# Down products of a feed-forward network in the seven-product form, for 18 of 22 feature tiles

## The chip, the cores and the metric

The kernel runs on one core of a Trainium2 chip. The metric is the device time of one execution in microseconds (us). TensorE (PE) multiplies, VectorE (DVE) and ScalarE (ACT) do elementwise work, GpSimd (POOL) here mostly issues DMAs that add what they bring to what is there, SyncE (SP) issues the plain loads.

## What is computed

A trunk of two layers over 512 positions of 1024 channels. Each layer has a feed-forward network (FFN), a mixer (pooling, a Fourier map and attention side by side) and a second FFN; a norm follows at the end. The change touches the FFNs alone:

```
def rmsnorm(x, g):
    y = xf * lax.rsqrt(jnp.mean(xf * xf, axis=-1, keepdims=True) + NORM_EPS)
    return (y * g.astype(jnp.float32)).astype(x.dtype)
def swiglu(x, w_gate, w_up, w_down):
    return (jax.nn.silu(x @ w_gate) * (x @ w_up)) @ w_down
...
for l in range(DEPTH):                       # 2
    h = rmsnorm(x, ffn1_norm[l])
    x = x + 0.5 * swiglu(h, ffn1_w_gate[l], ffn1_w_up[l], ffn1_w_down[l])
    ...
    h = rmsnorm(x, ffn2_norm[l])
    x = x + 0.5 * swiglu(h, ffn2_w_gate[l], ffn2_w_up[l], ffn2_w_down[l])
```

w_gate and w_up are 1024 x 2816, w_down is 2816 x 1024; all data is float32.

## The kernel before

**Operands in two halves.** Each float32 operand is split into a rounded part (hi, type float32r) and the rest (lo). A product is three matmuls: hi x hi, lo x hi, hi x lo (`mm3`, lines 106 to 109). `split` (102 to 104) makes hi on ACT and lo on DVE. Names: `hi`/`lo` are weights, `xh`/`xl`/`xo` the halves of the FFN's input, `ah`/`al` those of the hidden tiles.

**Layout.** x lies transposed in eight tiles of 128 channels x 512 positions. The hidden layer has 22 feature tiles of 128, handled in 11 pairs. `CHUNKS` (43) cuts the pairs into chunks of 4, 4 and 3. For each chunk the gate/up products of its pairs run first, and then the down products of its feature tiles into all eight output tiles, which are added to x (`ffn`, 577 to 602).

**The seven-product form.** A unit (class `Unit`, 448 to 510) is the gate and up product of one pair. The unit takes the input tiles in pairs too, and the 512 positions in two halves, so that gate and up are 2 x 2 block products, for which seven block products suffice instead of eight (Winograd's form of Strassen's). They are numbered 1 to 7; their inputs are the tiles themselves (1, 2, 3: `own` splits) and sums of tile halves (4 to 7: `ta`, `tb` in `joined`, 357 to 376), and their weights are sums of blocks too. Each product has 256 columns per matmul. They gather in four PSUM banks `qe`, `qa`, `qb`, `qg`. `head` runs products 5 and 1, `middle` 6, 7 and 2, `tail` 4 and 3; five DVE additions (`y`, `v`, `w`) combine the banks. The tail of a unit is written behind the head of the next one. The combined gate and up are multiplied with the norm's factor into tiles `t`, ACT applies silu, DVE multiplies gate with up (lines 506, 507; "gate" in the text), and `hidden` splits the result into `ah` and `al`.

**The plain down products.** For each output tile m one weight operand of up to 1024 columns is consumed, and every feature tile of the chunk costs three matmuls of 512 columns into bank `dn`; line 600 adds half of the bank to x. In the last chunk each finished output tile is fed to the next norm (`nxt.feed`): it makes that norm's operands and squares.

**Weights.** `raw` and `operand_of` write down, ahead of all, the loads and the operands in their order. SP loads a raw tile into one of 7 stage buffers; where a block sum is wanted, POOL adds a second block by an accumulating DMA (`plus`, line 167), and after an operand has been split, another (`then`, line 190) turns the stage tile into the next sum. `produce` splits a stage tile into one of four hi and four lo buffers; `operand` produces three operands ahead (`AHEAD`). So the hi and lo of an operand can be made only when PE has finished with the operand four before it.

**Order.** The program's order is not the code's: a scheduler interleaves the instructions of each engine, and each engine then runs its own list in order. Four hi and lo buffers, eight PSUM banks and one pool of 54 general tiles (`g`) bound how far it can go.

The lines that the change and the prediction's steps touch are 43, 122 to 155, 357 to 376, 448 to 532 and 577 to 602.

Of the kernel before, what the change touches and what calls it, by code (L numbers as in the profile page):

```python
# [32 lines left out]
P = 128  # L34
D = 1024
S = 512
# [6 lines left out]
CHUNKS = ((0, 4), (4, 8), (8, 11))  # L43
# [23 lines left out]
def build(tc, xt, gu, dn, qk, wv, wfa, wo, pw, fw, small, lamv, alibi, dft_c, dft_s, out):  # L67
# [3 lines left out]
    with (  # L71
# [50 lines left out]
        for l in range(L):  # L122
            for n in range(2):
                i = 2 * l + n
                if n:
# [3 lines left out]
                    for x in ORDER:  # L129
                        if x in src:  # L130
                            for z in range(2):
                                operand_of(raw(src[x][:, z * 1024 : (z + 1) * 1024]), eng=V if x in ON_VECTOR else None)
                for c0, c1 in CHUNKS:
                    tail = []
                    for u in range(c0, c1):
                        a11, a21, a22, a12 = [gu[i, u][:, q * 1024 : (q + 1) * 1024] for q in range(4)]
                        if not raws:
                            for x in (a11, a12, a21, a22):
                                operand_of(raw(x))
                            continue  # L140
                        t, t11 = raw(a21, plus=a22), raw(a11)
                        t12, t22 = raw(a12), raw(a22)
                        if u == 1 and i == 0:
                            for x, then in ((t11, a21), (t, a11), (t11, None), (t, a12), (t12, None)):
                                operand_of(x, then=then)
                            tail = [(t22, None), (t, None)]
                            continue
                        for x, then in [(t, a11), (t11, a21)] + tail + [(t, a12), (t11, None), (t12, None)]:
                            operand_of(x, then=then)
                        tail = [(t22, None), (t, None)]  # L150
                    for x, then in tail:
                        operand_of(x, then=then)
                    for m in range(KT):
                        w = 2 * (c1 - c0) * P
                        operand_of(raw(dn[i, m][:, 2 * c0 * P : 2 * c1 * P], w), w)
# [55 lines left out]
        X = [cp.tile([P, S], F32, name=f"x{k}") for k in range(KT)]  # L211
# [128 lines left out]

        class PairNorm(Norm):
# [15 lines left out]
            def joined(self, b1, b2, res=None):  # L357

                c0, c1 = slice(0, TH), slice(TH, S)
                ta, tb = g(name="ta"), g(name="tb")  # L360
# [641 lines left out]
```

## Time and profile before

| what | value |
|---|---|
| time, median of 3 runs | 1839.99 us (1838.53 to 1840.71) |
| the profiled execution's own time | 1840.45 us |
| its span, first to last instruction | 1838.7 us |
| mean granted TensorE clock | 0.987 |
| ACT, POOL busy | 884.9 us, 204.8 us |
| HBM read | 258.99 MB |

In the profile's rows the names stand as out<-in; "busy" adds the instructions of an engine, and "idle before" is the time its queue stood still just ahead of an instruction, with what released it. PE is the matmul row, PEld the loading of the stationary operand, which overlaps it. A matmul's own duration is modelled and overlaps the next one's, so distances between starts say more.

### The profile page before, as it was taken

What the parts mean: (1) busy time and instruction counts of PE and PEld (TensorE: products, weight loads), DVE (VectorE), ACT (ScalarE), POOL (GpSimd) and SP (SyncE); (2) the same over time, 40 slices, a digit from 0 to 9 for tenths busy, and PEclk for the clock granted to TensorE, in tenths of its full rate; (3) what the DMA queues carried; (4) which work ended last, traced back from release to release, by engine and by line L of the source; (5) the groups of instructions that cost most, each with busy time, mean ns of one, the idle gap of its engine ahead of it and who ended that gap; (6) DMA issues with size and microseconds to landing.
All of it is one profiled execution on the core that took longest, in us unless ns stands there. A gap on an engine that the chain in (4) does not pass through costs nothing.

```text
span 1838.7 us, 28135 instructions
## 1 busy us (share of the span) xinstructions
PE 1773.4 (96%) x11286; PEld 1602.7 (87%) x11286; DVE 1278.8 (70%) x2004; ACT 884.9 (48%) x1223; POOL 204.8 (11%) x242
## 2 busy tenths in 40 slices
PE   8999999999899999999999999999988999999997
PEld 7889989877678989989899899998766899899895
DVE  7765846868679765847887477477776887477474
ACT  7433424468646533424554244244875554244243
POOL 1101001001101101001010010100111110010101
PEclk9999999999899999999999999999998999999998
DMA  7757757545625857857677586665444467586661
GB/s 240 184 149 161 197 133 175 143 124 131 138 67 130 192 160 154 202 130 179 152 169 188 136 195 173 138 169 155 115 118 104 102 158 188 133 200 162 140 158 46
DMA packets 81778, 279.69 MB, mean 152 GB/s; under 512 B 9200, under 2 KB 12784, under 8 KB 81648
## 3 DMA queue, kind: packets, MB, share of 16 engines
q0 software_dynamic: 29376, 106.97, 33.6%
q1 hardware_dynamic: 48528, 166.73, 28.0%
q10 hardware_dynamic: 3744, 4.21, 0.8%
q8 instruction: 88, 1.44, 0.3%
q14 instruction: 42, 0.34, 0.1%
HBM read 258.99 MB, written 2.10 MB: 142 GB/s over the span
## 4 chain that ended last, share of the span: by engine, by line
PE 79%; DVE 6%; ACT 5%; DMA 4%; issue 4%; POOL 1%; SPq 0%; ACTq 0%; DVEq 0%; POOLq 0%
PE dn L107 8%; PE dn L108 8%; PE dn L109 8%; PE qg L462 4%; PE qg L464 4%; PE qg L463 4%; PE qe L463 4%; PE qe L464 4%; PE qe L462 4%; PE qa L464 4%; PE qa L463 4%; PE qa L462 4%; DMA st<-in_gu 4%; PE qb L463 2%; PE qb L464 2%
## 5 line engine op out<-in xcount | busy, mean ns | idle before, releaser
L103 ACT ACTIVATE hi<-st 128x1024 fp32r<-128x1024 f32 (+2 forms) x420 | 432.9, 1035 | 621.4 <-PE dn L108 223.6
L104 DVE TENSOR_TENSOR lo<-st,hi 128x1024 fp32r<-128x1024 f32 (+2 forms) x420 | 500.7, 1194 | 194.5 <-ACT hi L103 193.0
L108 PE MATMUL dn<-al,hi 128*128 128x512 f32 x704 | 274.6, 390 | 0.0
L109 PE MATMUL dn<-ah,lo 128*128 128x512 f32 x704 | 274.2, 389 | 0.0
L107 PE MATMUL dn<-ah,hi 128*128 128x512 f32 x704 | 271.9, 392 | 0.5
L462 PE MATMUL qg<-xh,hi 128*128 128x256 f32 x688 | 196.9, 286 | 6.1 <-ACT hi L103 3.2
L462 PE MATMUL qe<-xh,hi 128*128 128x256 f32 x688 | 196.9, 286 | 4.3 <-DVE nv L328 2.3
L463 PE MATMUL qg<-xh,lo 128*128 128x256 f32 x688 | 196.1, 285 | 0.9 <-DVE lo L104 0.9
L464 PE MATMUL qg<-xl,hi 128*128 128x256 f32 x688 | 196.1, 285 | 0.0
L464 PE MATMUL qe<-xl,hi 128*128 128x256 f32 x688 | 195.6, 284 | 0.1
L463 PE MATMUL qe<-xh,lo 128*128 128x256 f32 x688 | 195.4, 284 | 0.0
L190 POOL DMA_DIRECT2D st<-in_gu x129 | 116.1, 901 | 673.1 <-DVE lo L104 600.3
L600 DVE SCALAR_TENSOR_TENSOR x<-dn,x 128x512 f32<-128x512 f32 x96 | 66.2, 690 | 168.6 <-PE dn L109 168.6
L107 PEld LDWEIGHTS dn<-ah,hi 128*128 128x128 f32 x704 | 131.3, 188 | 31.9 <-ACT ah L103 5.9
L108 PEld LDWEIGHTS dn<-al,hi 128*128 128x128 f32 x704 | 132.2, 188 | 29.0 <-DVE al L104 2.4
L109 PEld LDWEIGHTS dn<-ah,lo 128*128 128x128 f32 x704 | 132.2, 188 | 26.9
L462 PEld LDWEIGHTS qg<-xh,hi 128*128 128x128 f32 x688 | 133.3, 194 | 7.4 <-ACT hi L103 3.4
L462 PEld LDWEIGHTS qe<-xh,hi 128*128 128x128 f32 x688 | 132.4, 192 | 8.1 <-ACT hi L103 4.9
L463 PEld LDWEIGHTS qg<-xh,lo 128*128 128x128 f32 x688 | 133.5, 194 | 1.1 <-DVE lo L104 1.1
L463 PEld LDWEIGHTS qe<-xh,lo 128*128 128x128 f32 x688 | 132.6, 193 | 1.3 <-issue 0.7
L464 PEld LDWEIGHTS qg<-xl,hi 128*128 128x128 f32 x688 | 133.4, 194 | 0.0
L464 PEld LDWEIGHTS qe<-xl,hi 128*128 128x128 f32 x688 | 132.6, 193 | 0.4 <-DVE xl L104 0.3
(274 smaller groups left out, 3923.3 us busy)
## 6 DMA issues: line engine op xcount, KB each, us to landing
st<-in_gu SPq DMA_DIRECT2D x175, 512.0 KB, 4.6
st<-in_gu POOLq DMA_DIRECT2D x172, 512.0 KB, 5.7
st<-in_dn SPq DMA_DIRECT2D x64, 512.0 KB, 4.2
lo<-st POOLq DMA_DIRECT2D x32, 512.0 KB, 5.0
st<-in_dn SPq DMA_DIRECT2D x32, 384.0 KB, 3.2
st<-in_qk SPq DMA_DIRECT2D x16, 512.0 KB, 3.7
st<-in_wo SPq DMA_DIRECT2D x16, 512.0 KB, 3.8
st<-in_wv SPq DMA_DIRECT2D x8, 512.0 KB, 4.9
```

The lines of the kernel that those rows point to most:

```text
L103: A.activation(hi, src, AF.Copy)
L104: (lo_eng or V).tensor_tensor(lo, src, f(hi), SUB)
L107: T.matmul(o, lh, rh, start=start, stop=False)
L108: T.matmul(o, lh, rl, start=False, stop=False)
L109: T.matmul(o, ll, rh, start=False, stop=stop)
L190: G.dma_start(t[:, 0:w], then, accum_op=ADD)
L462: T.matmul(o, wh[:, s], xh, start=start and p == 0 and z == 0, stop=False, **k)
L463: T.matmul(o, wl[:, s], xh, start=False, stop=False, **k)
L464: T.matmul(o, wh[:, s], xl, start=False, stop=stop and p == NK - 1 and z == 1, **k)
L600: V.scalar_tensor_tensor(X[m], b, 0.5, X[m], MUL, ADD)
```

## The change

The down products of the first nine pairs (18 of 22 feature tiles) take the seven-product form as well. `CHUNKS` becomes three chunks of three pairs and one of two; the last one keeps the plain down products. For a chunk of three pairs two `DownUnit`s run, each of four output tiles: the pairs of feature tiles are what the input pairs are in gate/up, and the two halves of positions are the same. So each product has 3 pairs x 2 x 3 = 18 matmuls of 256 columns, and a chunk has two units of seven products where it had eight plain operands.

- For each pair, the two hidden tiles are no longer split as `ah` and `al`, but made into the inputs of the seven products (`joined`: four half sums, then splits of `ta`, `tb` and the tiles).
- The unit ahead of the down products is written differently (`flush`): its gate and split are done by halves of positions, in the order in which they become ready.
- The first `DownUnit` of a chunk (`all_but_tail`) runs product 1, product 5 of the first two pairs, product 2, product 5 of the last pair, then 6 and 7. Its tail comes behind the head of the second one, and the tail of the second behind the head of the next chunk's first gate/up unit.
- Each `DownUnit` combines its banks by the same five additions and updates x by four additions of 2 x 256 columns.
- The weights of the down products are packed like those of gate/up: four blocks of 768 columns per unit, four loads and four accumulating DMAs, and seven splits of 768 columns, where a plain output tile had one load and one split.
- Two x tiles share one allocation (`XW`).

```
-CHUNKS = ((0, 4), (4, 8), (8, 11))
+CHUNKS = ((0, 3), (3, 6), (6, 9), (9, 11))
+NSEVEN = 9
...
+                def seven(src, w, plain=False, flush=False, special=False):
+                    nonlocal tail
+                    a11, a21, a22, a12 = src
...
+                    if flush:
+                        t11, t = raw(a11, w), raw(a21, w, a22)
+                    else:
+                        t, t11 = raw(a21, w, a22), raw(a11, w)
+                    t12, t22 = raw(a12, w), raw(a22, w)
...
+                    elif flush:
+                        use = tail + [(t11, a21), (t, a11), (t12, None), (t, a12), (t11, None)]
+                    else:
+                        use = [(t, a11), (t11, a21)] + tail + [(t, a12), (t11, None), (t12, None)]
+                    for x, then in use:
+                        operand_of(x, raws[x][1], then=then)
+                    tail = [(t22, None), (t, None)]
...
+                    if c1 <= NSEVEN:
+                        for o in range(2):
+                            q0 = [2 * P * (NSEVEN * q + c0) for q in range(4)]
+                            seven([d7[i, o][:, q : q + w] for q in q0], w, False, o == 0)
+                        continue
...
+        def own(b1, b2, res):
+            c0, c1 = slice(0, TH), slice(TH, S)
+            if b1 is not None:
+                one = g(F32R, name="xo")
+                split(b1[:, c0], one[:, c0], one[:, c1])
+                res[1] = one[:, c0], one[:, c1]
+            if b2 is not None:
+                hi, lo = g(F32R, name="xh"), g(F32R, name="xl")
+                split(b2, hi, lo)
+                res[2], res[3] = (hi[:, c0], lo[:, c0]), (hi[:, c1], lo[:, c1])
...
             def tail(self):
                 self.product(self.qg, 4, False, True)
-                w21, w12 = g(name="w21"), g(name="w12")
-                V.tensor_tensor(w21, self.qg, self.y, SUB)
-                V.tensor_tensor(self.t[1][:, :, 0:TH], halves(w21), self.r[0], MUL)
-                a1 = self.hidden(self.t[1])
+                w = g(name="w")
+                V.tensor_tensor(w, self.qg, self.y, SUB)
+                V.tensor_tensor(self.t[1][:, :, 0:TH], halves(w), self.r[0], MUL)
+                self.gated(1, slice(0, TH if self.flush else S))
+                if self.flush:
+                    own(None, self.t[1][:, 0], self.res)
+                elif not self.seven:
+                    a1 = self.hidden(1)
                 self.product(self.qe, 3, False, True)
...
+                self.gated(0, slice(TH if self.flush else 0, S))
+                if self.flush:
+                    self.act.append(joined(self.t[0][:, 0], self.t[1][:, 0], self.res))
+                elif self.seven:
+                    self.act.append(joined(self.t[0][:, 0], self.t[1][:, 0]))
+                else:
+                    self.act += [self.hidden(0), a1]
+
+            def gated(self, z, c):
+                t = self.t[z]
+                A.activation(t[:, 0, c], t[:, 0, c], AF.Silu)
+                V.tensor_tensor(t[:, 0, c], t[:, 0, c], t[:, 1, c], MUL)
...
+        class DownUnit(Unit):
...
+            def all_but_tail(self):
+                n = len(self.x)
+                self.qe, self.qa = bank("qe"), bank("qa")
+                self.product(self.qa, 1, True, True)
+                self.first()
+                w5 = operand()
+                self.product(self.qe, 5, True, True, w5, ps=range(n - 1))
+                self.product(self.qa, 2, False, True)
+                self.update(0, 0, self.qa)
+                self.product(self.qe, 5, True, True, w5, ps=[n - 1])
+                self.qb, self.qg = bank("qb"), bank("qg")
+                self.product(self.qb, 6, True, True)
+                self.product(self.qg, 7, True, True)
+                self.sums()
+                self.update(1, 1, self.v)
+            def update(self, j, c, src):
+                x = XW[2 * self.o + j][:, :, c * TH : (c + 1) * TH]
+                V.scalar_tensor_tensor(x, halves(src), 0.5, x, MUL, ADD)
...
+                    unit = Unit(nm, act, seven, seven and u == c1 - 1)
...
+                if seven:
+                    down = [DownUnit(o, act) for o in range(2)]
+                    down[0].all_but_tail()
+                    down[1].head()
+                    down[0].tail()
+                    down[1].middle()
+                    last = down[1]
+                    continue
```

How the engines' lists change is shown at one place, the end of a chunk, where the last unit's hidden tiles are finished and the down products begin. On DVE before, from the sum that follows product 4 of the chunk's last unit (`w` from bank `qg`) to the first update of x (`lo` are halves of coming weights, L507 is the gate):

```order
L497 TENSOR_TENSOR w_194_2475<-qg_2346,y_2405 128x512
L498 TENSOR_TENSOR t_2442<-w_194_2475,r_690 128x2x256
L104 TENSOR_TENSOR lo_2488<-st_2307,hi_2487 128x1024
L104 TENSOR_TENSOR lo_2526<-st_2347,hi_2525 128x1024
L507 TENSOR_TENSOR t_2442<-t_2442 128x512
L104 TENSOR_TENSOR al_2482<-t_2442,ah_2481 128x512
L501 TENSOR_TENSOR w_195_2476<-qe_2208,y_2405 128x512
L502 TENSOR_TENSOR t_2441<-w_195_2476,r_690 128x2x256
L507 TENSOR_TENSOR t_2441<-t_2441 128x512
L104 TENSOR_TENSOR al_2520<-t_2441,ah_2519 128x512
L600 SCALAR_TENSOR_TENSOR x_81<-dn_2529,x_81 128x512
```

The same place now (L562 is the gate, L549 the sum behind product 3; `xl` of `xh_3294` belongs to the second tile's own halves, `ta` and `tb` are the half sums of the last pair):

```order
L541 TENSOR_TENSOR w_3289<-qg_3152,y_3061 128x512
L542 TENSOR_TENSOR t_3248<-w_3289,r_684 128x2x256
L107 TENSOR_TENSOR lo_3301<-st_3096,hi_3300 128x768
L562 TENSOR_TENSOR t_3248<-t_3248 128x256
L549 TENSOR_TENSOR y_3061<-qe_3002,y_3061 128x512
L107 TENSOR_TENSOR lo_3349<-st_2934,hi_3348 128x768
L107 TENSOR_TENSOR xl_3295<-t_3248,xh_3294 128x512
L550 TENSOR_TENSOR t_3247<-y_3061,r_684 128x2x256
L107 TENSOR_TENSOR lo_3374<-st_2903,hi_3373 128x768
L562 TENSOR_TENSOR t_3247<-t_3247 128x256
L377 TENSOR_TENSOR ta_3332<-t_3247 128x256
L378 TENSOR_TENSOR ta_3332<-t_3247,t_3248 128x256
```

Before, two weight halves stood among the two gates and splits; now there are three, the gates are done by halves, and the two half sums `ta` come behind all of it, with their own splits still behind them. ACT's list at the same place now has the two weight splits `hi_3348` and `hi_3373` (products 6 and 7) ahead of `xh_3294`, the second tile's own split:

```order
L106 ACTIVATE hi_3300<-st_3096 128x768
L561 ACTIVATE t_3248<-t_3248 128x256
L106 ACTIVATE hi_3348<-st_2934 128x768
L106 ACTIVATE hi_3373<-st_2903 128x768
L106 ACTIVATE xh_3294<-t_3248 128x512
L561 ACTIVATE t_3247<-t_3247 128x256
L106 ACTIVATE xh_3338<-ta_3332 128x512
```

Before, ACT had two weight splits there and then only the silu and the splits of the two hidden tiles.

On PE before, behind product 3 of that unit, 35 matmuls of the down products stand whose inputs belong to earlier units, and then these (the last hidden tiles are `ah_2519` and `ah_2481`; 2529, 2562 and 2594 are three output tiles):

```order
L107 MATMUL dn_2594<-ah_2100,hi_2487 128x512
L108 MATMUL dn_2594<-al_2101,hi_2487 128x512
L109 MATMUL dn_2594<-ah_2100,lo_2488 128x512
L107 MATMUL dn_2529<-ah_2519,hi_2413 128x512
L107 MATMUL dn_2562<-ah_2519,hi_2447 128x512
L107 MATMUL dn_2594<-ah_2062,hi_2487 128x512
L108 MATMUL dn_2529<-al_2520,hi_2413 128x512
```

Now, behind product 3, the last pair's six matmuls of product 1 end, and products 6 and 7 of the first two pairs follow (`hi_3348`, `hi_3373`), 12 matmuls each, ahead of the first that needs the last pair's `ta`:

```order
L496 MATMUL qa_3347<-xo_3255,lo_3219 128x256
L497 MATMUL qa_3347<-xo_3255,hi_3218 128x256
L495 MATMUL qb_3424<-xh_2895,hi_3348 128x256
L495 MATMUL qg_3425<-xh_2891,hi_3373 128x256
L496 MATMUL qb_3424<-xh_2895,lo_3349 128x256
L497 MATMUL qb_3424<-xl_2896,hi_3348 128x256
```

Where the scheduler had down matmuls of three output tiles over three finished pairs to put behind product 3, it now has products of the two finished pairs alone, cut into pieces by their weights: one matmul of product 7 stands between the first and the second of product 6.

More of the change, by code (lines that the diff above doesn't have):

```diff
@@ L133, in build @@
                 for c0, c1 in CHUNKS:
-                    tail = []
                     for u in range(c0, c1):
[L136 to L150, printed above, removed]
+                        src = [gu[i, u][:, q * 1024 : (q + 1) * 1024] for q in range(4)]
@@ L210, in build @@
         nc.sync.dma_start(sm, small)
-        X = [cp.tile([P, S], F32, name=f"x{k}") for k in range(KT)]
+        XW = [cp.tile([P, 2, S], F32, name=f"x{k}") for k in range(NK)]
+        X = [XW[k // 2][:, k % 2] for k in range(KT)]
         load(1, NK)
@@ L448, in build, with __init__, product @@
         class Unit:
-            def __init__(self, nm):
-                self.nm = nm
-            def product(self, q, j, start, stop, w=None, ahead=True):
+            def __init__(self, nm, act=None, seven=False, flush=False):
+                self.nm, self.x, self.act, self.seven, self.flush = nm, nm.x, act, seven, flush
+            def product(self, q, j, start, stop, w=None, ahead=True, ps=None):
                 wh, wl = w or operand(ahead)
                 k = {"skip_group_check": True}
-                for p in range(NK):
-                    xh, xl = self.nm.x[p][j]
+                n = len(self.x)
+                for p in ps or range(n):
+                    xh, xl = self.x[p][j]
                     for z in range(2):
@@ L463, in product @@
                         T.matmul(o, wl[:, s], xh, start=False, stop=False, **k)
[L464 removed]
+                        T.matmul(o, wh[:, s], xl, start=False, stop=stop and p == n - 1 and z == 1, **k)
             def head(self):
@@ L523, in tail @@
             def tail(self, c):
-                res = []
-                for q in c:
-                    t = halves(wide("t"))
+                self.t = []
+                for z, q in enumerate(c):
+                    self.t.append(halves(wide("t")))
                     for i in range(2):
@@ L544, in begin @@
                 upto(4)
-                one, two = FirstUnit(nm), Unit(nm)
+                one, two = FirstUnit(nm, act, True), Unit(nm, act, True)
                 c0, c1 = one.head(), one.head()
@@ L561, in begin @@
                 sq = [nm.square(k) for k in range(KT)]
-                two.q1 = g(name="q1")
-                A.activation(two.q1, two.qa, AF.Copy)
+                two.first()
                 upto(7)
@@ L573, in begin @@
                 upto(11)
-                act += one.tail([c0, c1])
+                one.tail([c0, c1])
             return two
         def ffn(nm, nxt, first=False):
+            last = None
             for c0, c1 in CHUNKS:
-                act, last = [], None
+                act = []
+                seven = c1 <= NSEVEN
                 for u in range(c0, c1):
```

125 lines of the change are left out of this document (78 added, 47 removed).

## The prediction

> **What bounds the kernel now.** I read the engine table and the costliest groups of the page first, for the engine that never rests and for its waits.
>
> ```profile
> PE 1773.4 (96%) x11286; PEld 1602.7 (87%) x11286; DVE 1278.8 (70%) x2004; ACT 884.9 (48%) x1223; POOL 204.8 (11%) x242
> L107 PE MATMUL dn<-ah,hi 128*128 128x512 f32 x704 | 271.9, 392 | 0.5
> L462 PE MATMUL qg<-xh,hi 128*128 128x256 f32 x688 | 196.9, 286 | 6.1 <-ACT hi L103 3.2
> ```
>
> PE is busy 96% of the span. The last column is the idle time ahead of a group: 0.5 us for the first of the three down groups (704 matmuls each), 6.1 us for one of the gate/up groups. So inside the feed-forward networks (FFNs) PE hardly waits, chunk boundaries included, and time can only leave by fewer or shorter matmuls, or be added by new waits. The view by windows shows what stands beside PE in a plain down stretch and in a gate/up stretch (columns: window and its length, then busy us and instructions of PE, weight loads, DVE, ACT and POOL, then granted clock, DMA share, GB/s).
>
> ```profile
> 127.00:150.00 23.00, 23.00 (x103) 19.06 (x102) 7.67 (x8) 4.26 (x4) 3.45 (x4) 1.00 0.68 136
> 170.00:190.00 20.00, 20.00 (x169) 20.00 (x169) 16.79 (x21) 10.33 (x12) 3.45 (x4) 1.00 0.93 220
> ```
>
> The plain down products are where the others rest: DVE is busy 7.67 of 23 us there, against 16.79 of 20 us in gate/up, where the DMA engines are at 0.93. The change puts work like the second row in the place of the first.
>
> **What it removes: PE time.** A matmul's own duration overlaps its neighbours', so I take the distance between starts, from the timeline of PE.
>
> ```profile
> 124.20 0.39 PE L107 MATMUL dn<-ah,hi 128*128 128x512 f32 x1
> 127.83 0.39 PE L108 MATMUL dn<-al,hi 128*128 128x512 f32 x1
> ...
> 150.15 0.28 PE L463 MATMUL qe<-xh,lo 128*128 128x256 f32 x1
> 151.95 0.28 PE L463 MATMUL qe<-xh,lo 128*128 128x256 f32 x1
> ```
>
> Sixteen steps lie between the first two rows (3.63/16 = 0.2269 us for 512 columns), fifteen between the last two (1.80/15 = 0.1200 us for 256). For one pair of feature tiles and four output tiles the plain form takes 2 x 4 x 3 = 24 matmuls of 512, 5.45 us; the seven-product form 7 x 2 x 3 = 42 of 256, 5.04 us. An eighth of the columns goes, but only 0.406 us, 7%, of the time, since two narrow matmuls cost more than one wide one. There are 9 pairs x 2 units x 4 FFNs = 72 of these: **-29.2 us**. The order of the changed program has these matmuls (18 to a product, seven products to a unit), so the change does what it says.
>
> [...]
>
> **What it adds at the end of each three-pair chunk.** Before, the timelines of PE, DVE and ACT at one chunk's end show how long the last hidden tiles take.
>
> ```profile
> 231.64 0.28 PE L464 MATMUL qg<-xl,hi 128*128 128x256 f32 x1
> 231.76 0.28 PE L464 MATMUL qe<-xl,hi 128*128 128x256 f32 x1
> ...
> 231.97 0.69 DVE L497 TENSOR_TENSOR w<-qg,y 128x512 f32<-128x512 f32 x1 [2.51 <-PE qg L464]
> 232.69 0.69 DVE L498 TENSOR_TENSOR t<-w,r 128x512 f32<-128x512 f32 x1
> 233.30 2.35 DVE L104 TENSOR_TENSOR lo<-st,hi 128x1024 fp32r<-128x1024 f32 x2
> 235.57 0.68 DVE L507 TENSOR_TENSOR t<-t 128x512 f32<-128x512 f32 x1
> 237.56 0.68 DVE L501 TENSOR_TENSOR w<-qe,y 128x512 f32<-128x512 f32 x1
> ...
> 240.40 0.63 ACT L103 ACTIVATE ah<-t 128x512 fp32r<-128x512 f32 x1 [0.76 <-DVE t L507]
> ...
> 241.08 0.50 PE L107 MATMUL dn<-ah,hi 128*128 128x512 f32 x1
> ```
>
> From the end of the product into qg (231.76) to the last `ah` (241.03) 9.3 us pass; PE covers them with ten matmuls into qe (1.2 us) and 35 ready down matmuls of other outputs and pairs (7.9 us), and waits about 0.15 us. In the changed order the cover is shorter: 16 matmuls into qe, 6 of product 1, 12 of product 6, 12 of product 7, 46 x 0.12 = 5.5 us, before product 5 asks for the hi half of `ta` of the last pair. And DVE has more ahead of that: the rows shown with the change, w to the second `ta`. Their steps come from starts of like rows:
>
> ```profile
> 902.44 0.95 DVE L104 TENSOR_TENSOR lo<-st,hi 128x768 fp32r<-128x768 f32 x1
> 903.31 0.42 DVE L362 TENSOR_TENSOR ta<-xg,xg 128x256 f32<-128x256 f32 x1
> 903.64 0.95 DVE L104 TENSOR_TENSOR lo<-st,hi 128x768 fp32r<-128x768 f32 x1
> ...
> 907.68 0.69 DVE L104 TENSOR_TENSOR xl<-tb,xh 128x512 fp32r<-128x512 f32 x1
> 908.28 0.69 DVE L104 TENSOR_TENSOR xl<-xg,xh 128x512 fp32r<-128x512 f32 x1
> ```
>
> A step is 0.87 us for 768 columns, 0.33 for 256, 0.60 for 512 (0.72 where the next needs it, 231.97 to 232.69). DVE starts 0.21 us after PE (231.76 to 231.97). Then w 0.72, t 0.60, lo 0.87, gate 0.33, y 0.60, lo 0.87, xl 0.60, t 0.60, lo 0.87, gate 0.33, ta 0.33, ta 0.42 to its end: 7.1 us. With 0.3 us of waits on ACT in between (xl stands behind two weight splits in ACT's queue, the ta behind the gate) and ACT's split, 0.63 us by the `ah` row and 0.04 to each side, `ta` is there 8.4 us after the qg product: **2.9 us of wait**. The next need, the lo half of `ta`, stands behind the two `tb` and its own 0.69 on DVE, ready at 9.2 us, while PE has 0.5 us of matmuls: 0.4 more. Earlier in the boundary product 5 starts 12 matmuls (1.44 us) after the last product of the third unit frees its weight slot, and DVE first has t, xl and lo (0.60 + 0.60 + 0.87, from 0.3 on, to 2.4): 0.9 more. In all 4.2 us, at 3 boundaries x 4 FFNs: **+50.4 us**. From below: no waits on ACT, no early wait and none for the lo half, 2.6 us (31); from above: two waits of 0.7 as at the `ah` above and DVE 1 us late on arrival, 6.6 us (79). I take the middle, since it is counted row by row.
>
> [...]
>
> **What it adds elsewhere on DVE.** A gate/up unit loses two `al` (2 x 0.60) and gains four half sums, one 256 and three 512 splits (4 x 0.33 + 0.12 + 0.33 + 1.8): +2.4 us on 16.8 in 20. A down unit has 7 splits of 0.87, five sums and four updates of 0.60 to 0.72, some 12 us beside 126 x 0.12 = 15.1 us of PE. Both fit under PE, with 0.8 and 3 us to spare: zero, and a rival below.
>
> **FFN ends.** The last chunk now has two pairs, 96 matmuls (21.8 us) instead of 144 (32.7), over the same eight updates and feeds on DVE. The rows are the first update, DVE's last split and PE's last down row at the end of layer 0, then the same places with the first mixer matmul ahead of the first mixer.
>
> ```profile
> 899.22 0.69 DVE L600 SCALAR_TENSOR_TENSOR x<-dn,x 128x512 f32<-128x512 f32 x1 [1.51 <-PE dn L109]
> 920.56 0.39 PE L109 MATMUL dn<-ah,lo 128*128 128x512 f32 x1
> 932.88 0.68 DVE L104 TENSOR_TENSOR xl<-xg,xh 128x512 fp32r<-128x512 f32 x1
> ...
> 346.61 0.69 DVE L600 SCALAR_TENSOR_TENSOR x<-dn,x 128x512 f32<-128x512 f32 x1 [1.51 <-PE dn L109]
> 368.19 0.39 PE L107 MATMUL pp<-xh,hi 128*128 128x512 f32 x1
> 370.66 0.74 DVE L310 SCALAR_TENSOR_TENSOR xl<-x,sm,xh 128x512 fp32r<-128x512 f32 x1
> ```
>
> At the first, DVE ends 12.8 us after PE (933.6 against 920.8). Now the first update comes some 15 us ahead of PE's end instead of 21.6, and DVE has 34.4 - 1.1 = 33.3 us from there (four splits 0.27 narrower), so it ends 18.3 us after: **+5.5 us** once (0 if other products cover it, 11 if PE waits for all of the shorter chunk). At the two mixers DVE ends some 7.6 us after PE instead of 3.2, under the 42 matmuls (9.5 us) ahead of the last feature tile: about 0. The plain chunk's own boundary has 24 narrow and 22 wide matmuls, 7.9 us, for a chain of about 8.2: 0.3 x 4, with as much again for the mixers **+3 us** (0 to 8).
>
> **The sum.** The profiled execution took 1840.45 us, half a microsecond over the median of 1839.99. 1840.45 - 29.2 + 50.4 + 5.5 + 3 = **1870 us**; with the bounds 1842 to 1909.
>
> **Rivals.** *The boundary is covered.* If the last pair comes within about 1 us of need, 12 us stand against 29.2, and with 3 us for the rest the time is 1826. For it: before, PE waited only 0.15 us on the same chain. Against: the cover falls from 9.1 to 5.5 us while DVE's rows grow. It turns the sign where a boundary costs less than 1.7 us ((29.2 - 8.5)/12). 12%.
>
> *The DMA queues run late.* The page's queue part and issues, and one PE wait of before:
>
> ```profile
> q0 software_dynamic: 29376, 106.97, 33.6%
> q1 hardware_dynamic: 48528, 166.73, 28.0%
> st<-in_gu POOLq DMA_DIRECT2D x172, 512.0 KB, 5.7
> ...
> 1519.21 0.39 PE L462 MATMUL qg<-xh,hi 128*128 128x256 f32 x1 [1.10 <-DVE w L483]
> ```
>
> The 172 accumulates of this row and 32 more of its size share q0's 618 us: 3.0 us of all 16 engines each. The change adds 96 of three quarters of the size, 218 us; loads in q1 cost 1.6 us a half megabyte. So a gate/up unit takes 18.6 of 20.2 us of the DMA engines and a down unit 14 of 15.1, without the rest of the plain stretch. If two waits like the one quoted come in each chunk, 26 us are added: 1896. 14%.
>
> *DVE binds in gate/up.* With 0.9 us lost in two units of each chunk, 22 us: 1892. Against it stand three operands of lead on the weights. 10%.
>
> The forecast keeps 64%. Its lower edge reaches no change, which here means within 0.2% (3.7 us), about what a measurement of this kernel can tell. Faster 0.13, same 0.06, slower 0.81; the range is 1832 to 1906, which leaves out the covered case and the far ends.
>
> **What would show it.** Right: down matmuls 0.120 us apart; twelve gaps of PE, about 3 us ahead of qe<-xh and about 1 us at product 5's first lo, released by DVE and ACT; PE busy less by some 29 us, idle more by some 59. Wrong: boundaries of 1 us, or gaps spread over all products with a DMA as releaser.

## The result and the profile after

The changed kernel takes 2050.39 us in the median (2045.63 to 2052.16 without the execution named next), the kernel before 1839.99: a ratio of 1.113 with an interval of 1.112 to 1.115, 210 us more. The profiled execution of that first measurement, 2187.59 us, ran at a granted clock of 0.752 wherever the others had 1.0 (0.745 in the mean); the profile shown here is that of a second measurement of the same kernel, 2052.04 us in the median, whose profiled execution took 2050.67 us at a clock of 0.953.

> The changed kernel once more, for a profile at the full granted clock. Its other executions took 2046 to 2052 us at a mean clock of 0.951 to 0.959, where 1870 us were forecast. Theory B (boundaries): the loss sits at the 12 chunk ends, so each has PE waits and half-clock stretches of some 20 us in all ((2046 - 1811) / 12). Theory D (DMA): the accumulating DMAs land late all through the chunks, so PE waits on weights in gate/up and in down units, the chain that ended last goes through DMA for over 15% of the span (4% before), and the DMA share stays at 0.9 or more. Theory C (clock): PE does not wait more than forecast (some 60 us), but the granted clock is under 1.0 over long stretches.

The page of the changed kernel, at the places that were shown of before (engines, queues, the chain that ended last, the costliest groups with the idle time ahead of them, and the DMA issues with their microseconds to landing):

```profile
PE 1836.3 (90%) x12582; PEld 1704.4 (83%) x12582; DVE 1510.5 (74%) x2500; ACT 983.5 (48%) x1447; POOL 287.8 (14%) x338
q0 software_dynamic: 43200, 144.72, 41.3%
q1 hardware_dynamic: 53136, 166.73, 25.4%
PE 34%; DMA 26%; DVE 18%; issue 12%; ACT 8%; POOL 1%; SPq 0%; ACTq 0%; POOLq 0%; DVEq 0%
L495 PE MATMUL qg<-xh,hi 128*128 128x256 f32 x976 | 303.8, 311 | 67.6 <-ACT hi L106 57.4
L496 PE MATMUL qg<-xh,lo 128*128 128x256 f32 x976 | 302.1, 309 | 23.7 <-DVE lo L107 23.7
L495 PE MATMUL qe<-xh,hi 128*128 128x256 f32 x976 | 281.1, 288 | 27.6 <-DVE v L518 20.3
...
st<-in_gu POOLq DMA_DIRECT2D x172, 512.0 KB, 7.6
st<-in_d POOLq DMA_DIRECT2D x96, 384.0 KB, 5.1
```

PE has sunk from 96% to 90% of a longer span. The idle time ahead of qg<-xh,hi was 6.1 us and is 67.6, and its releaser is a weight split on ACT. The chain that ended last was made up otherwise in the kernel before:

```profile
PE 79%; DVE 6%; ACT 5%; DMA 4%; issue 4%; POOL 1%; SPq 0%; ACTq 0%; DVEq 0%; POOLq 0%
```

PE was 79% of it and DMA 4%; now PE is 34%, DMA 26%, DVE 18%. So theory D's sign is there (over 15% for DMA); the table below shows that theory B's places, the boundaries, hold a part as well. The accumulating DMAs of the gate/up weights land 7.6 us after their issue, where they took 5.7.

**Where the time went.** From the starts of PE's matmuls one can add up, place by place, by how much the distance to the next start exceeds the bare step (0.120 us for 256 columns, 0.227 for 512; only excesses over 0.03 us are counted). In the feed-forward networks this lost time was 31.0 us before and is 270.2 us now. Take it from the spans and 1838.7 - 31.0 = 1807.7 us are left before, 2048.8 - 270.2 = 1778.6 after. So the fewer matmuls did save 29.1 us, and 239 us of new waits came on top. Their places:

| place | after, us | per occurrence |
|---|---|---|
| boundary: tail of the third unit, first down unit up to product 7 | 65.3 | 5.4, 12 times |
| rest of the down units | 29.8 | 2.5, 12 times |
| turn: products 6, 7 and 2 of the gate/up unit behind the down units | 93.5 | 7.3, 12 times, and 6.5 at the opening of the first network |
| head of the third gate/up unit (with the tail of the second) | 50.7 | 6.0 in the second and third chunk of each network, 8 times; 3.1 in the four first chunks together |
| the rest of the networks | 30.9 | |

Before, the places like the third and the fourth held 6.8 and 4.1 us. The 6.8 stand at the opening of the first network, ahead of product 7; the changed kernel loses 6.5 there, and some 6 us of this kind are in every figure given for the turn below but that of the last experiment. The twelve turns themselves hold 87.0. PE's timeline in the third chunk shows one of each; the bracket holds the wait and its releaser:

```profile
253.52 0.28 PE L497 MATMUL qb<-xl,hi 128*128 128x256 f32 x1
256.37 0.39 PE L495 MATMUL qg<-xh,hi 128*128 128x256 f32 x1 [2.57 <-ACT hi L106]
257.63 0.43 PE L496 MATMUL qg<-xh,lo 128*128 128x256 f32 x1 [0.87 <-DVE lo L107]
...
290.66 0.28 PE L497 MATMUL qa<-xo,hi 128*128 128x256 f32 x1
294.09 0.36 PE L495 MATMUL qe<-xh,hi 128*128 128x256 f32 x1 [3.15 <-DVE v L518]
...
295.74 0.58 PE L495 MATMUL qg<-xh,hi 128*128 128x256 f32 x1 [1.17 <-DVE v L519]
296.11 0.41 PE L496 MATMUL qg<-xh,lo 128*128 128x256 f32 x1
296.33 0.41 PE L497 MATMUL qg<-xl,hi 128*128 128x256 f32 x1
...
314.35 0.39 PE L496 MATMUL qe<-xh,lo 128*128 128x256 f32 x1 [1.30 <-DVE lo L107]
...
319.49 0.28 PE L497 MATMUL qg<-xl,hi 128*128 128x256 f32 x1
...
326.12 0.39 PE L496 MATMUL qg<-xh,lo 128*128 128x256 f32 x1 [0.60 <-DVE lo L107]
...
327.92 0.39 PE L495 MATMUL qe<-xh,hi 128*128 128x256 f32 x1 [0.23 <-ACT xh L106]
...
344.45 0.39 PE L495 MATMUL qg<-xh,hi 128*128 128x256 f32 x1 [0.79 <-ACT hi L106]
345.44 0.39 PE L496 MATMUL qg<-xh,lo 128*128 128x256 f32 x1 [0.61 <-DVE lo L107]
```

At 253.5 to 257.6 the turn waits for product 7's weights, at 290.7 to 295.7 the head of the third unit waits for DVE's `v` sums, 314 to 328 is the boundary, 344 the second down unit. Behind the two waits of 3.15 and 1.17 us the matmuls come 0.215 us apart (296.11, 296.33) instead of 0.120: the trace has the granted clock at 0.5 from 295.39 to 298.80.

**The turn.** The view by windows around it (columns: window, length, busy us of PE, weight loads, DVE, ACT and POOL, then granted clock, DMA share, GB/s), then ACT's, DVE's and POOL's timelines there:

```profile
240.00:245.00 5.00, 5.00 (x44) 5.00 (x43) 5.00 (x8) 0.85 (x1) 2.61 (x3) 1.00 0.82 173
245.00:250.00 5.00, 5.00 (x44) 5.00 (x43) 2.92 (x4) 1.54 (x2) 0.11 (x1) 1.00 1.02 226
250.00:255.00 5.00, 3.80 (x32) 3.60 (x30) 0.00 (x0) 0.00 (x0) 0.76 (x1) 1.00 1.03 247
255.00:260.00 5.00, 2.76 (x13) 2.56 (x14) 3.65 (x5) 3.90 (x4) 0.00 (x0) 0.78 0.63 156
```

```profile
247.28 1.06 ACT L106 ACTIVATE hi<-st 128x1024 fp32r<-128x1024 f32 x1 [5.55 <-DMA st<-in_gu]
255.26 3.90 ACT L106 ACTIVATE hi<-st 128x1024 fp32r<-128x1024 f32 x4 [6.43 <-DMA st<-in_gu]
...
248.37 1.23 DVE L107 TENSOR_TENSOR lo<-st,hi 128x1024 fp32r<-128x1024 f32 x1 [1.68 <-ACT hi L106]
256.35 1.23 DVE L107 TENSOR_TENSOR lo<-st,hi 128x1024 fp32r<-128x1024 f32 x1 [6.75 <-ACT hi L106]
...
240.52 0.86 POOL L209 DMA_DIRECT2D st<-in_gu  x1 [6.61 <-DVE lo L107]
243.53 1.21 POOL L209 DMA_DIRECT2D st<-in_gu  x1
249.89 0.86 POOL L209 DMA_DIRECT2D st<-in_gu  x1 [5.15 <-DVE lo L107]
```

A weight for product 7 is made in a circle over four engines: POOL's accumulating DMA can go only after DVE has split the operand before (240.52, after 6.61 us of waiting), ACT can split only what has landed, DVE only what ACT has split. From 245 to 255 the DMA engines are full (1.02, 1.03). The block sum issued at 243.53 lands 11.6 us later, ACT stands 6.43 us for it, four splits then come at once (255.26), and PE's qg follows at 256.37. All three engines run their lists in order, so the lateness of one transfer was handed on, as 6.75 us of waiting on DVE and 2.57 on PE.

### The profile page after: what moved, and what is told of

Its sections match the earlier page's. It is cut to its first block, busy times and chain, and to the rows that moved or that the text cites. A ratio compares the mean times of both kernels' runs of the same rounds, so it can differ in the third digit from the quotient of the medians.

```text
span 2185.7 us, 32007 instructions
## 1 busy us (share of the span) xinstructions
PE 2097.8 (96%) x12582; PEld 1907.7 (87%) x12582; DVE 1522.1 (70%) x2500; ACT 987.8 (45%) x1447; POOL 287.2 (13%) x338
## 4 chain that ended last, share of the span: by engine, by line
PE 66%; DMA 16%; DVE 7%; issue 6%; ACT 4%; POOL 1%; SPq 0%; ACTq 0%; POOLq 0%; DVEq 0%
DMA st<-in_gu 12%; PE qg L496 5%; PE qg L495 5%; PE qg L497 4%; PE qe L496 4%; PE qe L497 4%; PE qe L495 4%; DMA st<-in_d 4%; PE qa L496 4%; PE qa L495 4%; PE qa L497 4%; DVE lo L107 3%; PE pp L111 2%; PE pp L110 2%; PE pp L112 2%
## 5 line engine op out<-in xcount | busy, mean ns | idle before, releaser
L106 ACT ACTIVATE hi<-st 128x1024 fp32r<-128x1024 f32 (+3 forms) x524 | 490.4, 956 | 792.1 <-DMA st<-in_gu 204.4
L107 DVE TENSOR_TENSOR lo<-st,hi 128x1024 fp32r<-128x1024 f32 (+3 forms) x524 | 574.5, 1098 | 346.5 <-ACT hi L106 337.6
L495 PE MATMUL qg<-xh,hi 128*128 128x256 f32 x976 | 311.1, 319 | 14.6 <-ACT hi L106 11.4
L496 PE MATMUL qe<-xh,lo 128*128 128x256 f32 x976 | 310.0, 318 | 6.0 <-DVE lo L107 6.0
L497 PE MATMUL qe<-xl,hi 128*128 128x256 f32 x976 | 310.6, 318 | 0.4
L495 PE MATMUL qb<-xh,hi 128*128 128x256 f32 x488 | 154.8, 317 | 1.9
L497 PE MATMUL qb<-xl,hi 128*128 128x256 f32 x488 | 153.8, 315 | 2.0 <-DVE xl L107 2.0
L495 PE MATMUL qa<-xh,hi 128*128 128x256 f32 x488 | 154.3, 316 | 1.0 <-ACT hi L106 1.0
L496 PE MATMUL qb<-xh,lo 128*128 128x256 f32 x488 | 154.0, 316 | 0.4 <-DVE lo L107 0.4
L497 PE MATMUL qa<-xo,hi 128*128 128x256 f32 x488 | 154.4, 316 | 0.0
L496 PE MATMUL qa<-xh,lo 128*128 128x256 f32 x488 | 154.3, 316 | 0.0
L495 PE MATMUL qa<-xo,hi 128*128 128x256 f32 x488 | 153.7, 315 | 0.6 <-ACT hi L106 0.6
```

The source lines that it names most:

```text
L106: A.activation(hi, src, AF.Copy)
L107: (lo_eng or V).tensor_tensor(lo, src, f(hi), SUB)
L495: T.matmul(o, wh[:, s], xh, start=start and p == 0 and z == 0, stop=False, **k)
L496: T.matmul(o, wl[:, s], xh, start=False, stop=False, **k)
L497: T.matmul(o, wh[:, s], xl, start=False, stop=stop and p == n - 1 and z == 1, **k)
```

## Experiments

In all of them the kernel before ran beside on the same chip, at 1839.50 to 1841.83 us in the median. "Lost time" is the sum explained above.

**The chunks alone.** The kernel before with the new chunks, all down products plain.

```diff
-CHUNKS = ((0, 4), (4, 8), (8, 11))
+CHUNKS = ((0, 3), (3, 6), (6, 9), (9, 11))
```

> The kernel before with chunks of 3, 3, 3 and 2 pairs and plain down products: the chunking alone. Theories B and D: no or little loss, 1840 to 1850 us, since the plain down products cover a boundary and leave the DMA queues free. If the chunking itself costs, it is over 1860 us.

1866.49 us, ratio 1.014 (1.011 to 1.016), so 25 us, over the 1860 that was the mark for a cost of the chunking itself. The lost time grows from 31.0 to 54.2 us, 17 of these 23 us in the plain down stretches (4.2 to 21.0), where waits for `ah` and for the weights' `lo` appear. Shorter chunks cost something in the plain form, too. Of the 21.0 us 12.9 stand in the last chunk, of two pairs, a stretch that the changed kernel keeps and where it loses 1.8, so this is not a term of its 239 us. Another cost of the chunking is: the openings of the networks, behind that short chunk, lose 21.7 us here and 22.1 in the changed kernel, against 12.0 before.

**The boundary away.** The last pair's tiles are not used in the down products; the second pair's stand in their place.

```diff
-                    down = [DownUnit(o, act) for o in range(2)]
+                    down = [DownUnit(o, [act[0], act[1], act[1]]) for o in range(2)]
```

> The changed kernel, whose down units read the second pair's inputs in the place of the third pair's, so that no down product needs the chunk's last unit; all work stays. Theory B: most of the 235 us over the floor of 1811 us goes, to under 1880 us. Theory D: little goes (the 50 us that the forecast put at the boundaries at most), over 1980 us.

1957.11 us, ratio 1.063 (1.060 to 1.065): 95 us less than the changed kernel, and between the figures of theory B (under 1880) and theory D (over 1980). At the boundary 65.3 us of lost time become 16.7. That is what the last pair's chain costs there, 49 us. The other half of the gain is elsewhere: the turn falls from 93.5 to 54.2, the rest of the down units from 29.8 to 15.8. The head of the third unit stays at 53.9.

**The sums' DMAs away.** The down weights are loaded and split as before, without their 96 accumulating DMAs; the block sums of the down products are left out.

```diff
-                        t11, t = raw(a11, w), raw(a21, w, a22)
+                        t11, t = raw(a11, w), raw(a21, w, a22 if sums else None)
...
-                        operand_of(x, raws[x][1], then=then)
+                        operand_of(x, raws[x][1], then=then if sums else None)
...
-                            seven([d7[i, o][:, q : q + w] for q in q0], w, False, o == 0)
+                            seven([d7[i, o][:, q : q + w] for q in q0], w, False, o == 0, sums=False)
```

> The changed kernel without the 96 accumulating DMAs of the down units' weights (their block sums are left out, matmuls, splits and loads stay). Theory B: little changes, over 2000 us. Theory D: most of the loss goes, since the DMA work falls to that of before; with the boundaries as forecast some 1870 us, under 1900 us.

1963.80 us, ratio 1.066 (1.064 to 1.069): 88 us less, again between the two theories' figures. The rest of the down units falls from 29.8 us to nothing, the turn from 93.5 to 29.8. The boundary (62.5) and the third unit's head (54.9) stay. So the late weights are the down units' and the turn's trouble, and the turn belongs to the gate/up weights only in name: the transfers that delay it are those of the down units ahead of it.

```profile
L495 PE MATMUL qg<-xh,hi 128*128 128x256 f32 x976 | 290.6, 298 | 25.3 <-ACT hi L106 13.9
```

In this group of its page 57.4 us of waits for ACT's `hi` have become 13.9.

**Bytes, steps, or the accumulating form?** Two kernels with the same instructions in the same order: the down weights' accumulating DMAs at half their columns (half of the block sums left out), and at full size as plain DMAs from the same queue (the block brought last stands in place of the sum).

```diff
...
-                G.dma_start(t[:, 0:w], then, accum_op=ADD)
+                p = w if w == 1024 else w // 2
+                G.dma_start(t[:, 0:p], then[:, 0:p], accum_op=ADD)
```

> The changed kernel with the accumulating DMAs of the down weights cut to half their columns (384 of 768): half of the block sums of the down weights are left out; the number and order of all instructions stay. Theory W (at the turn from the down units to the next gate/up unit the 16 DMA engines are full, and the sums' bytes are what fills them): about half of the 88 us that leaving them all out gave, 2000 to 2015 us, and the wait at product 6 and 7 of the first gate/up unit falls from 93.5 us in all to some 60. Rival O (what counts is the number of steps in a row: split, then the add, then the next split, and POOL's list in order): little of it, 2035 us or more.

```diff
...
-                G.dma_start(t[:, 0:w], then, accum_op=ADD)
+                G.dma_start(t[:, 0:w], then, **({"accum_op": ADD} if w == 1024 else {}))
```

> The changed kernel with the 96 accumulating DMAs of the down weights made into plain DMAs of the same size, from the same queue, into the same place: the block sums are left out (the block brought last stands alone). Same bytes from HBM, same order, same number of steps. Theory W with the accumulating form as the dear part (3.1 us of the 16 engines for 512 KB against 1.6 for a plain load): close to half of the 88 us comes back, about 2010 us. Theory W with plain bytes as the price: 2030 to 2040. Rival O (steps in a row): 2040 or more.

Half the columns: 2019.40 us, ratio 1.095 (1.092 to 1.098), 33 us less, close to theory W's range in the time, though not at the turn, for which it had 60 us. Plain: 1975.93 us, ratio 1.071 (1.069 to 1.074), 76 us less, nearly all that leaving them out gives and more than any figure expected. So it is neither the number of steps nor the bytes from HBM, which the plain form keeps; it is the accumulating form. What such transfers take of the DMA engines comes from the queue rows, against the kernel without them (30.9% of 1960.5 us, 605.8 us). The rows are of the half-size and the plain kernel:

```profile
q0 software_dynamic: 43200, 125.85, 36.9%
```

```profile
q0 software_dynamic: 37056, 144.72, 37.3%
```

Full accumulates: (41.3% of 2048.8 - 605.8)/96 = 2.50 us of all 16 engines each; half: (36.9% of 2008.4 - 605.8)/96 = 1.41; plain: (37.3% of 1967.7 - 605.8)/96 = 1.34. In the lost time both cure the down units (29.8 to 4.3 and 0), but only the plain form cures the turn (88.1 against 29.9). Half and plain take nearly the same engine time, so engine time alone doesn't decide the turn. What differs is when the last down weight arrives. ACT's timelines at the second down unit's end, in the second chunk of the first network, half size and then plain:

```profile
229.77 3.48 ACT L106 ACTIVATE hi<-st 128x768 fp32r<-128x768 f32 x4 [3.24 <-DMA st<-in_d]
```

```profile
222.44 1.06 ACT L106 ACTIVATE hi<-st 128x1024 fp32r<-128x1024 f32 x1 [0.95 <-PE qe L497]
224.60 1.06 ACT L106 ACTIVATE hi<-st 128x1024 fp32r<-128x1024 f32 x1 [1.10 <-PE qb L497]
226.76 0.85 ACT L106 ACTIVATE hi<-st 128x768 fp32r<-128x768 f32 x1 [1.10 <-PE qg L497]
```

With the plain DMAs ACT waits only for PE to free a weight buffer, that is, it is ahead. With half-size accumulates it stands 3.24 us for a landing, and the splits for the next gate/up unit come behind it in one lump. By the trace, at this place the second sum of the second down unit lands 9.7 us after its issue in the changed kernel, 7.8 at half size, 4.3 plain; the first accumulate of the gate/up unit behind is issued 0.2 us before that unit's product 5 in the first two and 2.5 us before it in the plain kernel. What the turn loses goes by when the block sum for product 7 lands, counted from the start of that unit's product 5. Over the 124 turns of the changed kernel and ten of its variants (all the runs here but the one with the chunks alone): landed within 11 us, a turn loses at most 0.4 us; at 15 to 16 us it loses 6.1 to 7.9. From issue to landing this sum takes about the same time in both kernels, 12.2 us at half size and 11.4 plain in the mean; the issue is what moves, from 3.0 us after that start to 0.8. In two of the plain kernel's twelve turns it comes 1.7 and 2.3 us after it, and these two lose 4.2 and 7.3 us, as late turns of the other kernels do.

**Twelve transfers at the turn.** The block sum for the next gate/up unit (512 KB) stands in POOL's list ahead of three sums of the second down unit. Here these 12 are plain (the second block stands in place of the sum).

```diff
-                    G.dma_start(st[:, 0:w], plus, accum_op=ADD)
+                    turn = w == 1024 and pos[1] > 0 and raws[pos[1] - 1][1] == 768
+                    G.dma_start(st[:, 0:w], plus, **({} if turn else {"accum_op": ADD}))
```

> The changed kernel with 12 of its accumulating DMAs made plain: the block sum of the first gate/up unit behind each pair of down units (512 KB, issued ahead of the second down unit's own three sums in POOL's list); so the second block stands there in place of the sum. Same bytes, same order. Theory Q (the three down sums stand behind that transfer, and what it holds up passes on through ACT's, DVE's and POOL's lists): the last of them lands 8 us after its issue instead of 9.7, the waits of the second down unit's middle (24 us) mostly go and those of the first gate/up unit's middle (93 us) shrink by a third or more: 1990 to 2025 us. Rival E (what counts is the DMA engines' time in all): 12 transfers of 3.1 us become 1.6, 18 us at the very most and by the 74 us for 96 of three quarters some 12 us: 2033 to 2045 us.

2034.14 us, ratio 1.106 (1.105 to 1.108), 18 us less: rival E's figure. The landing behind it does fall as theory Q has it (9.7 to 7.6 us), and the rest of the down units loses half of its waits (29.8 to 13.7 us), but the turn keeps all of its own (97.3). The one transfer in front is not the cause of the turn.

**Both away.** Without the sums and without the last pair.

> The changed kernel without the sums of the down weights and without the third pair in the down products (its place is taken by the second): both left out together. If the two costs are apart (the boundary's hidden tiles, and the weights' DMAs), the gains add: 2050 - 93 - 88 = about 1870 us. If they are one slack that both draw on: 1900 to 1955. What is left in either case is the wait at the head of the third gate/up unit, 54 us in both single runs.

1921.08 us, ratio 1.0428 (1.0410 to 1.0445): 131 us less than the changed kernel, not 95 + 88. The two causes share some 50 us, in the turn and the down units, which either edit frees. Left are the turn with 24.0, the boundary with 16.6 and, untouched, the third unit's head with 54.3.

**The third unit's head.** DVE's timeline in the changed kernel ahead of the wait at 290.7:

```profile
277.78 1.22 DVE L107 TENSOR_TENSOR lo<-st,hi 128x1024 fp32r<-128x1024 f32 x1 [6.25 <-ACT hi L106]
...
285.06 0.68 DVE L517 TENSOR_TENSOR y<-qb,y 128x512 f32<-128x512 f32 x1
285.66 0.41 DVE L377 TENSOR_TENSOR ta<-t 128x256 f32<-128x256 f32 x1
...
292.66 0.68 DVE L107 TENSOR_TENSOR xl<-tb,xh 128x512 fp32r<-128x512 f32 x1
293.26 0.68 DVE L518 TENSOR_TENSOR v<-qe,y 128x512 f32<-128x512 f32 x1
```

The first of the second unit's sums stands at 285.06, the next (`v`) only at 293.26; between them lies the whole join of the first pair, with three weight splits. But DVE had also stood 6.25 us before all this, and order alone isn't enough: in the first chunks of the three later networks most of the same join stands between the same two sums, and PE loses next to nothing. There DVE begins `y` 8.2 to 10.3 us before PE's last start in the third unit's products 5 and 1, in the second and third chunks only 5.4 to 7.4 us. The windows of the second and the third unit show how unevenly DVE's work falls (columns as above):

```profile
264.90:285.00 20.10, 20.10 (x170) 20.10 (x169) 12.24 (x15) 7.88 (x10) 2.42 (x4) 1.00 0.84 196
285.00:311.30 26.30, 21.98 (x170) 21.60 (x169) 22.94 (x35) 13.03 (x19) 4.23 (x6) 0.94 0.82 174
```

The 22.94 us of DVE in the second row are more than the 20.2 us that the unit's 168 matmuls take at 0.120. One kernel leaves the first pair's join out (the second pair takes its place in the down products); another leaves nothing out and writes that join behind the second unit's sums.

```diff
-                    self.act.append(joined(self.t[0][:, 0], self.t[1][:, 0]))
+                    self.act.append(joined(self.t[0][:, 0], self.t[1][:, 0]) if self.act else None)
...
-                    down = [DownUnit(o, act) for o in range(2)]
+                    down = [DownUnit(o, [act[1], act[1], act[2]]) for o in range(2)]
```

> The changed kernel without the join of a chunk's first pair (4 half sums, 3 splits: 4.1 us of DVE per chunk), whose place in the down products is taken by the second pair: the first pair's part of the down products is left out. Theory V (at the head of the third gate/up unit PE waits for the second unit's v sums because DVE has the first pair's join ahead of them): the 51 us of waits there go, 1990 to 2005 us. Rival L (DVE is late there because it stood before, behind a weight split whose DMA was late, 6.25 us in the third chunk): less than a third of it goes, 2030 us or more.

```diff
...
                     unit.middle()
+                    if seven and u == c0 + 1 and not act:
+                        last.join()
                     last = unit
```

> The changed kernel, nothing left out: the join of a chunk's first pair is written behind the second unit's sums, so that in DVE's list the v sums stand ahead of all but the first half sum of the join. Theory V (the order in DVE's list makes PE wait at the third unit's head): the 51 us of waits there fall under 15, and the time by 20 to 45 us, 2005 to 2030. Rival B (DVE has no room in that stretch, whatever the order): the waits move to the next place, 2040 or more.

Without the join: 2028.91 us, ratio 1.101 (1.099 to 1.103), 23 us less; the lost time at the third head goes from 50.7 to 3.7 us, but the boundary takes 94.4 instead of 65.3. With the late join: 2038.85 us, ratio 1.108 (1.103 to 1.114), 13 us less, though its executions lie between 2026.75 and 2052.76, so that this gain is hardly clear of noise; the third head goes to 3.4, the boundary grows to 104.9. The late join's DVE timeline, at the same place:

```profile
283.10 0.68 DVE L517 TENSOR_TENSOR y<-qb,y 128x512 f32<-128x512 f32 x1
...
284.83 0.68 DVE L518 TENSOR_TENSOR v<-qe,y 128x512 f32<-128x512 f32 x1
...
293.51 0.69 DVE L107 TENSOR_TENSOR xl<-tb,xh 128x512 fp32r<-128x512 f32 x1
```

Here `v` follows `y` after one weight split, and PE does not wait. So theory V is right about the place: with DVE as late as it is there, the order of its list makes that wait, and rival L, by which little of the wait would go, is not. Theory V is wrong about the time, where both runs missed its range. Rival B is right about it: DVE has no room, and most of what is freed turns up at the next place where PE needs DVE, the boundary.

**All three away.** No sums, no join of the first pair, and the second pair in the place of the first and third.

> The changed kernel without the sums of the down weights, and with the second pair in the place of the first and the third in the down products (the first pair is not joined): block sums and two thirds of the distinct hidden tiles are left out of the down products. PE's matmuls and all loads stay. If the three costs (sums' DMAs, boundary, the join ahead of the v sums) are the whole of the loss, what the run without the first two left, 1921 us, falls by the 54 us of waits at the third unit's head: 1865 to 1880. If the DVE time given back turns up as a wait elsewhere, as in the run without the join alone: about 1898. Either way above 1840 minus 29: the rest is the chunking (25 us in the plain kernel) and the turns.

1863.43 us, ratio 1.014 (1.010 to 1.017). All matmuls and all plain loads are still there, and 189 of the 210 us are gone; the lost time is 82.0 us: boundary 29.5, turn 12.3 (half of it at the opening of the first network), third head 2.5, the rest of the down units nothing.

```profile
L495 PE MATMUL qg<-xh,hi 128*128 128x256 f32 x976 | 281.2, 288 | 6.7 <-ACT hi L106 5.3
```

The wait ahead of this group, 67.6 us in the changed kernel, is about what it was before the change (6.1).

**One such chunk in each network.** Chunks of three, four and four pairs, and the seven-product form for the first one only; nothing is left out.

```diff
-CHUNKS = ((0, 3), (3, 6), (6, 9), (9, 11))
-NSEVEN = 9
+CHUNKS = ((0, 3), (3, 7), (7, 11))
+NSEVEN = 3
...
```

> The seven-product form for the first three pairs of each network alone (chunks of 3, 4 and 4 pairs, the two later ones plain): 4 chunks of the new kind instead of 12, three chunks per network as before. If the loss hangs on each such chunk (boundary, down units, turn to the next gate/up unit, third unit's head: 210 + 29 = 239 us over 12, 20 us each): 1840 - 10 + 80 = about 1910 us. If it comes from the traffic that builds up over chunks in a row, or from the shorter chunks (25 us in the plain kernel): 1840 to 1870.

1932.50 us, ratio 1.050 (1.048 to 1.052), 22 us over the figure for a cost per chunk. Boundary (6.5 us each) and turn (8.2 us each, without the opening) cost per chunk no less than with twelve of them (5.4 and 7.3), so these two do not build up over chunks in a row. The third unit's head can't be told from this kernel: it costs only in chunks that have down units ahead of them, and the one new chunk of a network has none (4.7 us in all). What comes on top of the forecast lies in the plain chunks behind (the last unit's tail and the plain stretch, 28 us of the 135.0 of lost time), where nothing was expected. No version with the seven-product form beat the kernel before.

## Why the prediction was wrong

The sign was right, and the size was off by a factor of seven: +30 us were forecast, the range ended at 1906, and it became +210.

- **PE time, -29.2 us: right.** Without the lost time the spans differ by 29.1 us, and with one chunk in each network by 1807.7 - (1932.3 - 135.0) = 10.4 us, where a third of 29.2 is 9.7.
- **The boundary, +50.4 us: right in place, too small by a quarter.** It measures 65.3 us. The chain itself came out as counted: from the last start into qg (319.49, plus a step of 0.12) to the first matmul with the last pair's `ta` (327.92) it takes 8.3 us, where 8.4 stood. The early wait is 1.30 us instead of 0.9, and the waits in between are ahead of products 6 and 7, for weight splits that stand in ACT's and DVE's lists among the last pair's rows, rather than in one piece ahead of qe<-xh.
- **FFN ends and the rest, +8.5 us: about right in sum.** The rest of the networks' lost time rose from 31.0 - 6.8 - 4.1 = 20.1 us to 30.9. Most of it stands at one place, the opening of the third network (behind the end of layer 0), where 2.6 us became 11.6 and 5.5 more were forecast; the 3 us for the plain chunks' boundaries and the mixers don't show.
- **"A gate/up unit ... A down unit ... Both fit under PE, with 0.8 and 3 us to spare: zero": the step that failed.** In its place stand 93.5 - 6.8 us at the turn, 29.8 in the down units and 50.7 - 4.1 at the third unit's head, 163 us. As sums DVE and the DMA engines did fit, DVE over two units at least: 12.24 + 22.94 = 35.2 us beside 336 matmuls of 0.120, 40.3 us; but the work came in the second of the two. They did not fit in order: each weight passes POOL, DMA, ACT and DVE one after the other, each of these runs its list in order, and three operands of lead are three products, which a down unit shortens from 2.88 to 2.16 us each (24 and 18 matmuls of 0.12). The accumulating DMAs land 5 to 14 us after their issue there. The runs show it from both sides: without the 96 sums 88 us go, with the same bytes as plain transfers 76, and leaving out the join of one pair frees 47 us at one place and gives 29 of it back at another.
- **The rivals "The DMA queues run late" (1896) and "DVE binds in gate/up" (1892): both right in mechanism, both under-priced, and they came together.** The first was priced at two waits of 1.1 us in each chunk, from a row of the kernel before; the turn and the down units lose 9.7 us in each. The price came from a kernel in which the queue had slack (landing 5.7 us after issue in the middle, where it became 7.6).
- **No term for the clock.** In the networks PE's matmuls without any wait, but at half the clock, cost 52 us of the 270 by the same count, against 4 of the 31 before. The trace shows 36 stretches at 0.5, 195.6 us in all, against 9 and 51.6 before. In the experiments on the changed kernel the mean granted clock of the profiled execution was 0.954 to 0.981, highest where the lost time was least (82.0 us, all three away).

What is open: why the chain at the turn starts later behind half-size accumulates than behind plain ones, though both take about 1.4 us of the DMA engines. That the start decides what the turn loses is read from the traces; no run moved it alone. Nor is it shown what makes DVE late at the third unit's head, which loses as much without the sums' DMAs. More stage buffers or a longer lead were not tried.

## What to carry to other kernels

A sum of busy times that fits under the bounding engine says only that a cost could be hidden: here zero was forecast so, and 163 us came. Where an operand passes several in-order engines one after the other, count its chain against the lead that the buffers give, above all where the change shortens the steps that make up this lead, and do not price a queue that the change fills by the waits it shows today. Freeing one engine's order, here, moved most of a wait only as far as the next place that asks the same engine (the late join: 47.3 us less at the third unit's head, 39.6 more at the boundary).

## What the runs showed of the hardware

- **The accumulating DMAs took about twice what plain ones took.** 384 KB cost 2.50 us of all 16 DMA engines with the addition and 1.34 without, from the same queue; the median landing fell from 5.1 to 3.8 us. In one such burst, of gate/up sums, the other queue all but stood still: between 245 and 247.5 us the trace starts 127 packets of q0 and 2 of q1, though a load that SP had issued at 244.05 was under way until 252.79.
- **Half the clock behind waits.** In the changed kernel the stretches at a granted clock of 0.5 are 3.41 us long or a multiple of it (but for the last, at the program's end). In the 3.41 us just ahead of each PE stood idle for about 1.0 us or more by the matmuls' rows, but all through them ahead of only three of the 36; ahead of the stretch at 500.19 us it was two waits, of 1.05 and 0.93 us. Within them the matmuls of 256 columns start 0.215 us apart, where 0.120 is the bare step. No run shows how much idle time brings such a stretch on.
